# Dense peer experts: 48 first products ahead of the loop instead of 20, a third of all results kept in DRAM, and a gate stage without data work on GpSimd

## The chip, the cores and the metric

One core of a Trainium2 chip runs the whole program. The metric is the device time of one execution in microseconds (us). Five engines work side by side, each in its own order: TensorE (PE, with its weight loads as PEld), VectorE (DVE), ScalarE (ACT), GpSimd (POOL), and SyncE (SP), which here only starts transfers. Sixteen DMA engines move data between DRAM and the on-chip memory.

## The reference, cut to what matters

The program is two transformer blocks, one after the other, over 512 tokens of width 1024. The change lies in one part of the first block, the product-key layer `peer`:

```python
q = (nf @ w_q).reshape(t, PEER_HEADS, D_KEY)
...
v1, i1 = lax.top_k(s1, TOPK)
v2, i2 = lax.top_k(s2, TOPK)
...
idx = (e1 * N_KEYS + e2).reshape(t, PEER_HEADS * TOPK)
gates = jax.nn.softmax(vals.astype(jnp.float32), axis=-1).astype(n.dtype)
...
    ug = expert_u[ib]
    act = jax.nn.gelu(jnp.einsum("td,tkd->tk", xb, ug)) * gb
    vg = expert_v[ib]
    return jnp.einsum("tk,tkd->td", act, vg)
```

Each token picks 128 of 16384 small experts (8 heads, 16 each). An expert is a row of `expert_u` and a row of `expert_v`. The token's output is the sum over its experts of gelu(token . u) times the gate times v.

## The kernel before, in words

The kernel treats 384 of the 512 tokens (TD = 384, three tiles of 128) densely: it computes the product with all 16384 experts and multiplies by a gate matrix that is zero for the experts that a token did not choose. The experts are taken in 128 groups of 128. The last 128 tokens are treated sparsely: for each of the 128 chosen experts of every token, a gather fetches the rows (one indirect DMA of 128 rows of 4 KB, started by POOL; 128 gathers of u and then 128 of v), and DVE works on each.

All float32 products are split in a high and a low part: ACT writes the high part, the low part is the difference (`split`, L162), and three matmuls are summed (`mm3`, L175). The 16 top-k selections come first. Then these stages follow:

- **First products, S(e)** (`dense_s`, L693): load u of group e (tile ur), split it to uh and ul, 24 matmuls into a bank s, and gelu on ACT into a tile gl of [128 experts, 384 tokens]. Twenty of them (LAG) are made ahead of the loop: S(0) to S(7) as soon as the top-k is over, with the low part on POOL, six more between the gate calls, and six behind them.
- **Gate stage** (`decode`, `keys`, `gates`, L635 to L729): for each block of 4 tokens, DVE builds a one-hot tile gb (L717), and the weighted one-hot tile ga comes from a comparison on DVE for 8 tokens (eq, L710), times the gate, which is done by ACT (L722, four instructions) for three blocks in eight and by POOL (L724) for the other five. Four float32 matmuls (two PE instructions each) give the gate values of 4 tokens for all experts; ACT copies them into stg (L728). After eight blocks stg is stored to DRAM as gd (L729). There are 12 such calls, 96 blocks, 768 PE instructions.
- **Dense loop** (L565) over e = 0 to 127: **second product V(e)** (`dense_v`, L731) loads v of group e, splits it, multiplies gl[e] by the gates (gt, loaded from gd for four e at a time, L568), splits the result and adds 18 matmuls to six accumulators; then S(e + 20), while there is one; then gathers, so many that all 256 are through after 108 iterations (GSPAN). In this loop the order of the DVE instructions is the written one (`manual_schedule`). Elsewhere a scheduler, in the compiler, fixes each engine's order from the order of the program and its own estimate of times.

The first V needs the gates of all 12 calls. On SP all loads and the stores of gd stand in one queue. Buffers that matter: ur 3, uh 2, ul 2, ga 4, gb 2, bank s 2, bank b 4, vr 3, vh 2, vl 2, gr (gather) 4, gt 2.

Of the kernel before, what the change touches and what calls it, by code (L numbers as in the profile page):

```python
# [7 lines left out]
F32 = mybir.dt.float32  # L8
F32R = mybir.dt.float32r
BF = mybir.dt.bfloat16  # L10
I32 = mybir.dt.int32
U32 = mybir.dt.uint32
AF = mybir.ActivationFunctionType
# [5 lines left out]
T, D, NT, ND8 = 512, 1024, 4, 8  # L19
DT = 3  # L20
TD = DT * 128
LAG = 20
GSPAN = 108
GACT = (0, 3, 6)
NRAW, NRAW2 = 14, 3
CK, NSP, NDEP, POOLN = 2, 8, 5, 12
HEADS, TOPK, NK = 8, 16, 128
# [119 lines left out]
class Body:  # L147
# [331 lines left out]
    def peer(self, xst):  # L479
        tc, nc, A = self.tc, self.nc, self.A  # L480
        hT = self.hT
        gd = self.dram.tile([TD // 32, 128, 128, 32], F32, name="gd")
        with ExitStack() as st:
            pool = lambda **k: st.enter_context(tc.tile_pool(**k))
            np_ = pool(name="nhl", bufs=1)
# [20 lines left out]
                    nc.scalar.activation(n3[:, 512 * c:512 * c + 512], ps, AF.Copy)  # L506
            self.gl = {}
            S = lambda e, eng=None: self.dense_s(up, e, nh, nl, eng)
            ns = 0
            with tc.tile_pool(name="tk", bufs=1) as tk:  # L510
                v16 = tk.tile([128, 8, 4, 2, 16], F32, name="v16")
                i16 = tk.tile([128, 8, 4, 2, 16], U32, name="i16")
                w16 = tk.tile([128, 8, 4, 16], F32, name="w16")
                c16 = tk.tile([128, 8, 4, 16], U32, name="c16")
                with tc.tile_pool(name="p1", bufs=1) as p1, tc.tile_pool(name="p0", bufs=1) as p0:
                    for h in range(HEADS):
                        self.topk(p1, h, *self.xhl, v16, i16, w16, c16, (lambda: norm(p0)) if h == 0 else None)
                xst.close()
                ust = ExitStack()
                up = ust.enter_context(tc.tile_pool(name="up", bufs=1, side="right"))  # L520
                while ns < 8:
                    S(ns, nc.gpsimd)
                    ns += 1
                with tc.tile_pool(name="pg", bufs=1) as pg:
                    self.iota8 = pg.tile([128, 128, 8], BF, name="iota8")
                    nc.vector.tensor_copy(self.iota8, self.iota.rearrange("p (k o) -> p k o", o=1).to_broadcast([128, 128, 8]))
                    dec = self.decode(pg, i16, w16, c16, g3)
                    for t in range(NT):
                        tr = self.keys(pg, t, *dec, ix3)
                        if t < DT:  # L530
                            for q in range(4):
                                self.gates(pg, gd, 4 * t + q, tr, q)
                                if ns < LAG and q % 2:
                                    S(ns, nc.gpsimd if ns % 2 else None)
                                    ns += 1
            mst.close()
            while ns < LAG:
                S(ns)
                ns += 1
            with tc.tile_pool(name="pv", bufs=1) as pv:  # L540
                ast = ExitStack()
                ast.enter_context(self.banks(a=2 * DT))
                acc = [[self.bank("a") for c in range(2)] for t in range(DT)]
                dots = pv.tile([128, 128], F32, name="dots")
                o3 = pv.tile([128, 1024], F32, name="o3")
                scr = pv.tile([128, 1024], F32, name="scr")
                nc.vector.memset(o3, 0.0)

                def gather(j):
                    r = pv.tile([128, 1024], F32, name="gr", bufs=4)  # L550
                    if j == 128:
                        nc.scalar.activation(dots, dots, AF.Gelu_apprx_tanh)
                        nc.vector.tensor_mul(dots, dots, g3)
                    src, i = (A["u_r"], j) if j < 128 else (A["v_r"], j - 128)
                    nc.gpsimd.indirect_dma_start(out=r, out_offset=None, in_=src,  # L555
                                                 in_offset=bass.IndirectOffsetOnAxis(ap=ix3[:, i:i + 1], axis=0))
                    if j < 128:
                        nc.vector.tensor_tensor_reduce(scr, r, n3, op0=ALU.mult, op1=ALU.add, scale=1.0,  # L558
                                                       scalar=0.0, accum_out=dots[:, i:i + 1])
                    else:  # L560
                        nc.vector.scalar_tensor_tensor(o3, r, dots[:, i:i + 1], o3, op0=ALU.mult, op1=ALU.add)  # L561

                ng = 0
                with tc.manual_schedule(engines={mybir.EngineType.DVE}):
                    for e in range(128):  # L565
                        if e % 4 == 0:
                            gt = pv.tile([128, TD // 32, 4, 32], F32, name="gt", bufs=2)
                            nc.sync.dma_start(gt, gd[:, :, e:e + 4, :].rearrange("h p e t -> p h e t"))  # L568
                        self.dense_v(pv, e, gt, acc)
                        if e + LAG < 128:  # L570
                            S(e + LAG)
                        while ng < 256 and ng * GSPAN < 256 * (e + 1):
                            gather(ng)
                            ng += 1
                ust.close()
                self.early()

                for t in (3, 0, 1, 2):
                    if t < DT:
                        o = pv.tile([128, 1024], F32, name="gr", bufs=4)  # L580
                        for c in range(2):
                            nc.scalar.activation(o[:, 512 * c:512 * c + 512], acc[t][c], AF.Copy)
                    else:
                        o = o3
                    for c in range(2):
                        ps = self.bank("s")
                        for k in range(4):
                            i = 4 * c + k
                            nc.tensor.transpose(ps[:, 128 * k:128 * k + 128], o[:, 128 * i:128 * i + 128], self.ident)
                        h = hT[:, 4 * c:4 * c + 4, 128 * t:128 * t + 128]  # L590
                        nc.vector.tensor_add(h, h, ps.rearrange("p (k t) -> p k t", k=4))
                ast.close()
# [100 lines left out]
    def dense_s(self, up, e, nh, nl, eng=None):  # L693
        nc, A = self.nc, self.A
        uh, ul = self.load_split(up, [128, 8, 128], A["u_t"][e], "u", eng=eng)
        ps = self.bank("s")
        self.mm3(ps[:, :TD], lambda k: (uh[:, k], ul[:, k], nh[:, k, :TD], nl[:, k, :TD]), 8)
        g = up.tile([128, TD], F32, name="gl", bufs=LAG + 2)
        nc.scalar.activation(g, ps[:, :TD], AF.Gelu_apprx_tanh)
        self.gl[e] = g  # L700

    def gates(self, p, gd, th, tr, q):
        nc = self.nc
        tr, trb = tr
        stg = p.tile([128, 128, 32], F32, name="stg", bufs=2)
        for b in range(8):
            if b % 2 == 0:
                t = 32 * q + 4 * b
                eq = p.tile([128, 128, 8], BF, name="eq", bufs=3)
                nc.vector.tensor_tensor(eq, self.iota8, trb[:, t:t + 8].rearrange("p (o t) -> p o t", o=1).to_broadcast([128, 128, 8]),  # L710
                                        op=ALU.is_equal)
            t = 32 * q + 4 * b
            e = eq[:, :, 4 * (b % 2):4 * (b % 2) + 4]
            a = p.tile([128, 4, 128], F32, name="ga", bufs=4)
            bb = p.tile([128, 4, 128], F32, name="gb", bufs=2)
            ps = self.bank()
            nc.vector.tensor_tensor(bb, self.iota.rearrange("p (o k) -> p o k", o=1).to_broadcast([128, 4, 128]),  # L717
                                    tr[:, 1, t:t + 4].rearrange("p (t o) -> p t o", o=1).to_broadcast([128, 4, 128]),
                                    op=ALU.is_equal)
            if b % 8 in GACT:  # L720
                for i in range(4):
                    nc.scalar.activation(a[:, i], e[:, :, i], AF.Copy, scale=tr[:, 2, t + i:t + i + 1])  # L722
            else:
                nc.gpsimd.tensor_mul(a, e.rearrange("p k t -> p t k"),  # L724
                                     tr[:, 2, t:t + 4].rearrange("p (t o) -> p t o", o=1).to_broadcast([128, 4, 128]))
            for i in range(4):
                nc.tensor.matmul(ps[:, 128 * i:128 * i + 128], bb[:, i], a[:, i], start=True, stop=True)  # L727
            nc.scalar.activation(stg[:, :, 4 * b:4 * b + 4], ps.rearrange("p (t e) -> p e t", t=4), AF.Copy)  # L728
        nc.sync.dma_start(gd[th], stg)  # L729

    def dense_v(self, p, e, gt, acc):  # L731
# [811 lines left out]
```

## Time and profile before

| what | value |
|---|---|
| median of 3 runs | 3362.38 us (3360.96 to 3362.39) |
| the profiled execution, its own time | 3356.17 us |
| its span, first to last instruction | 3354.4 us |
| PE busy, share of the span | 94% |
| DVE / ACT / POOL busy | 80% / 52% / 30% |
| mean granted TensorE clock | 0.974 |
| gate stage with its first products, first S to first V | 365.0 to 635.6 us |
| dense loop | 635.6 to about 1607 us |

The stages are read by windows of the span, counted from its start; a busy share is that of one stretch, and the clock is the share of full speed that was granted in it. A busy PE is not always a PE at its peak, as the ends of matmuls are modelled; the spacing of the starts tells more than the length.

### The profile page before, as it was taken

What the parts mean: (1) busy time and instruction counts of PE and PEld (TensorE: products, weight loads), DVE (VectorE), ACT (ScalarE), POOL (GpSimd) and SP (SyncE); (2) the same over time, 40 slices, a digit from 0 to 9 for tenths busy, and PEclk for the clock granted to TensorE, in tenths of its full rate; (3) what the DMA queues carried; (4) which work ended last, traced back from release to release, by engine and by line L of the source; (5) the groups of instructions that cost most, each with busy time, mean ns of one, the idle gap of its engine ahead of it and who ended that gap; (6) DMA issues with size and microseconds to landing.
All of it is one profiled execution on the core that took longest, in us unless ns stands there. A gap on an engine that the chain in (4) does not pass through costs nothing. (4 is left out here: it accounts for less than half of the span.)

```text
span 3354.4 us, 44364 instructions
## 1 busy us (share of the span) xinstructions
PE 3139.9 (94%) x15489; PEld 2645.6 (79%) x15489; DVE 2679.3 (80%) x4138; ACT 1756.8 (52%) x2297; POOL 1014.4 (30%) x617
## 2 busy tenths in 40 slices
PE   8999877999999999999999898999999999999995
PEld 6777776899999999998777665777777777777774
DVE  8968889677777777775756745999998999999995
ACT  4232366433333333333545433677777777777774
POOL 0004355344444444440444213222222222222221
PEclk9999888999999999999999998999999999999998
DMA  4342223788888988984211335899999999999994
GB/s 139 98 132 78 85 120 161 293 305 304 301 304 299 309 305 299 306 283 150 101 61 41 104 105 200 321 341 334 337 340 348 339 343 336 334 339 344 339 343 152
DMA packets 280244, 819.30 MB, mean 244 GB/s; under 512 B 29648, under 2 KB 91984, under 8 KB 278224
## 3 DMA queue, kind: packets, MB, share of 16 engines
q1 hardware_dynamic: 223760, 659.09, 55.2%
q0 software_dynamic: 46080, 151.04, 13.8%
q10 hardware_dynamic: 10176, 6.29, 0.6%
q8 instruction: 123, 2.02, 0.2%
q14 instruction: 105, 0.86, 0.1%
HBM read 782.74 MB, written 50.33 MB: 248 GB/s over the span
## 5 line engine op out<-in xcount | busy, mean ns | idle before, releaser
L180 PE MATMUL s<-nh,uh 128*128 128x384 f32 x1024 | 350.4, 342 | 9.7 <-ACT uh L163 9.6
L182 PE MATMUL s<-nh,ul 128*128 128x384 f32 x1024 | 349.2, 341 | 3.4 <-POOL ul L164 2.7
L181 PE MATMUL s<-nl,uh 128*128 128x384 f32 x1024 | 348.0, 340 | 0.0
L163 ACT ACTIVATE vh<-vr 128x1024 fp32r<-128x1024 f32 x128 | 135.9, 1062 | 311.3 <-issue 291.3
L555 POOL DMA_INDIRECT gr<-in_u_r_dram,ix x128 | 192.4, 1503 | 260.6 <-DVE dots L558 222.9
L555 POOL DMA_INDIRECT gr<-in_v_r_dram,ix x128 | 195.4, 1527 | 250.0 <-DVE o L561 218.4
L745 PE MATMUL a<-vh,gh 128*128 128x512 f32 x768 | 236.6, 389 | 0.0
L745 PE MATMUL a<-vl,gh 128*128 128x512 f32 x768 | 236.4, 389 | 0.0
L745 PE MATMUL a<-vh,gll 128*128 128x512 f32 x768 | 236.3, 389 | 0.0
L164 DVE TENSOR_TENSOR ul<-ur,uh 128x1024 fp32r<-128x1024 f32 x117 | 144.4, 1234 | 100.3 <-ACT uh L163 100.3
L164 DVE TENSOR_TENSOR vl<-vr,vh 128x1024 fp32r<-128x1024 f32 x128 | 156.6, 1224 | 67.7 <-ACT vh L163 67.7
L180 PEld LDWEIGHTS s<-nh,uh 128*128 128x128 f32 x1024 | 195.7, 191 | 14.7 <-ACT uh L163 10.5
L163 ACT ACTIVATE gh<-gl 128x384 fp32r<-128x384 f32 x128 | 67.3, 526 | 262.6 <-DVE gl L736 262.6
L182 PEld LDWEIGHTS s<-nh,ul 128*128 128x128 f32 x1024 | 195.0, 190 | 4.7 <-POOL ul L164 3.7
L181 PEld LDWEIGHTS s<-nl,uh 128*128 128x128 f32 x1024 | 195.2, 191 | 4.0
L163 ACT ACTIVATE uh<-ur 128x1024 fp32r<-128x1024 f32 x128 | 135.2, 1056 | 75.6 <-PE s L181 62.6
L745 PEld LDWEIGHTS a<-vl,gh 128*128 128x128 f32 x768 | 144.2, 188 | 30.2
L745 PEld LDWEIGHTS a<-vh,gll 128*128 128x128 f32 x768 | 144.2, 188 | 29.9
L561 DVE SCALAR_TENSOR_TENSOR o<-gr,dots,o 128x1024 f32<-128x1024 f32 x128 | 164.1, 1282 | 3.8 <-DMA gr<-in_v_r_dram,ix 1.2
L558 DVE CUSTOM_DVE_ANT_0 scr<-gr,n 128x1024 f32<-128x1024 f32 x128 | 156.4, 1222 | 4.8 <-DMA gr<-in_u_r_dram,ix 2.3
L727 PE MATMUL b<-ga,gb 128*128 128x128 f32 x768 | 118.8, 315 | 44.2 <-DVE gb L717 34.8
L745 PEld LDWEIGHTS a<-vh,gh 128*128 128x128 f32 x768 | 142.6, 188 | 21.4
(6594 smaller groups left out, 9342.5 us busy)
## 6 DMA issues: line engine op xcount, KB each, us to landing
wr<-in_w_dram SPq DMA_DIRECT2D x768, 512.0 KB, 6.1
ur<-in_u_t_dram SPq DMA_DIRECT2D x128, 512.0 KB, 5.0
vr<-in_v_r_dram SPq DMA_DIRECT2D x128, 512.0 KB, 6.7
gd<-stg SPq DMA_DIRECT2D x12, 2048.0 KB, 6.9
gt<-gd SPq DMA_DIRECT2D x32, 768.0 KB, 9.4
wqr<-in_w_q_dram SPq DMA_DIRECT2D x16, 512.0 KB, 3.6
wir<-in_w_in_dram SPq DMA_DIRECT2D x15, 512.0 KB, 3.6
wlr<-in_w_in_dram SPq DMA_DIRECT2D x12, 512.0 KB, 3.7
```

Of the source, the lines that this page charges most:

```text
L163: self.nc.scalar.activation(hi, raw, AF.Copy)
L164: (eng or self.nc.vector).tensor_sub(lo, raw, hi.bitcast(F32))
L180: mm(ps, ah, bh, start=(k == 0 and start), stop=False)
L181: mm(ps, ah, bl, start=False, stop=False)
L182: mm(ps, al, bh, start=False, stop=(k == n - 1 and stop))
L555: nc.gpsimd.indirect_dma_start(out=r, out_offset=None, in_=src, in_offset=bass.IndirectOffsetOnAxis(ap=ix3[:, i:i + 1], axis=0))
L558: nc.vector.tensor_tensor_reduce(scr, r, n3, op0=ALU.mult, op1=ALU.add, scale=1.0, scalar=0.0, accum_out=dots[:, i:i + 1])
L561: nc.vector.scalar_tensor_tensor(o3, r, dots[:, i:i + 1], o3, op0=ALU.mult, op1=ALU.add)
L727: nc.tensor.matmul(ps[:, 128 * i:128 * i + 128], bb[:, i], a[:, i], start=True, stop=True)
L745: mm(acc[t][c], a[:, ts], v[:, 512 * c:512 * c + 512], start=(e == 0 and a is gh and v is vh), stop=(e == 127 and a is gl))
```

## The change

Forty-eight first products are made ahead of the loop. The groups 1, 4, 7, ... 118 (SPILL, 40 of 128) are all among them; the result of such a one is stored to a DRAM tensor gsd by a DMA that ACT starts, and loaded again by SP just ahead of its V, into one of three tiles gs. Of the other 88 (KEEP), the first 8 are made ahead and stay on chip as before. The first 8 of the 48 come right after the top-k, the other 40 are handed out one at a time behind single blocks of the gate stage (slots for 42, by `ahead`). No low part and no ga is made on POOL any more: the low part of u is always made on DVE; ga is made on ACT for four blocks in eight (from eq, 24 of which are left of 48) and on DVE for the other four (four `tensor_scalar` of [128, 128] each). In the loop only 80 S are left, none in the iterations of SPILL. Gathers are paced by the products done (128 V and 80 S, 208 in all) and are through after 88% of them.

```diff
-LAG = 20
-GSPAN = 108
-GACT = (0, 3, 6)
+LAG = 8
+SPILL = range(1, 120, 3)
+KEEP = [e for e in range(128) if e not in SPILL]
+GSPAN = 0.88
+GACT = (0, 1, 4, 5)
...
+        self.gsd = self.dram.tile([len(SPILL), 128, TD], F32, name="gsd")
...
+            it = iter([e for e in range(128) if e in SPILL or e in KEEP[:LAG]])
+            def ahead(b, q):
+                if b in ((0, 3, 6) if q % 2 else (0, 2, 4, 6)):
+                    e = next(it, None)
+                    if e is not None:
+                        S(e)
...
-                while ns < 8:
-                    S(ns, nc.gpsimd)
-                    ns += 1
+                for _ in range(8):
+                    S(next(it))
...
-                                self.gates(pg, gd, 4 * t + q, tr, q)
-                                if ns < LAG and q % 2:
-                                    S(ns, nc.gpsimd if ns % 2 else None)
-                                    ns += 1
+                                self.gates(pg, gd, 4 * t + q, tr, q, ahead)
...
-            while ns < LAG:
-                S(ns)
-                ns += 1
+            for e in it:
+                S(e)
...
+                ng, done, total = 0, 0, 128 + len(KEEP) - LAG
+                later = iter(KEEP[LAG:])
...
+                        if e in SPILL:
+                            self.gl[e] = up.tile([128, TD], F32, name="gs", bufs=3)
+                            nc.sync.dma_start(self.gl[e], self.gsd[SPILL.index(e)])
                         self.dense_v(pv, e, gt, acc)
-                        if e + LAG < 128:
-                            S(e + LAG)
-                        while ng < 256 and ng * GSPAN < 256 * (e + 1):
+                        done += 1
+                        s = next(later, None) if e in KEEP else None
+                        if s is not None:
+                            S(s)
+                            done += 1
+                        while ng < 256 and ng * GSPAN * total < 256 * done:
                             gather(ng)
...
+        if e in SPILL:
+            g = up.tile([128, TD], F32, name="gsp", bufs=3)
+            nc.scalar.activation(g, ps[:, :TD], AF.Gelu_apprx_tanh)
+            nc.scalar.dma_start(self.gsd[SPILL.index(e)], g)
+            return
...
-            if b % 2 == 0:
-                t = 32 * q + 4 * b
-                eq = p.tile([128, 128, 8], BF, name="eq", bufs=3)
+            if b in GACT and b % 2 == 0:
+                eq = p.tile([128, 128, 8], BF, name="eq", bufs=2)
...
-            if b % 8 in GACT:
-                for i in range(4):
-                    nc.scalar.activation(a[:, i], e[:, :, i], AF.Copy, scale=tr[:, 2, t + i:t + i + 1])
-            else:
-                nc.gpsimd.tensor_mul(a, e.rearrange("p k t -> p t k"),
-                                     tr[:, 2, t:t + 4].rearrange("p (t o) -> p t o", o=1).to_broadcast([128, 4, 128]))
+            for i in range(4):
+                if b in GACT:
+                    nc.scalar.activation(a[:, i], eq[:, :, 4 * (b % 2) + i], AF.Copy, scale=tr[:, 2, t + i:t + i + 1])
+                else:
+                    nc.vector.tensor_scalar(a[:, i], self.iota, tr[:, 0, t + i:t + i + 1], tr[:, 2, t + i:t + i + 1],
+                                            op0=ALU.is_equal, op1=ALU.mult)
...
+            ahead(b, q)
```

## Rows read from the trace of the kernel before

**Rows 1.** Tile vh: the matmuls of the loop; ns min/median/max, first and last start us.

```profile
L745 PE MATMUL a<-vh,gh x768: 389/389/391, 635.7 to 1606.8; 128*128 128x512 f32 x192
```

**Rows 2.** Windows: length; PE, PEld, DVE, ACT, POOL busy (instructions); clock; DMA share; GB/s.

```profile
400.00:600.00 200.00, 156.92 (x1029) 144.33 (x1028) 166.22 (x162) 126.56 (x253) 111.69 (x63) 0.88 0.34 136
650.00:1500.00 850.00, 850.00 (x4331) 777.74 (x4330) 656.79 (x784) 309.43 (x413) 374.62 (x246) 1.00 0.89 303
1550.00:1600.00 50.00, 50.00 (x222) 41.42 (x221) 27.59 (x37) 19.46 (x25) 0.00 (x0) 1.00 0.47 148
```

**Rows 3.** Groups of instructions, 360 to 640 us; busy us, mean ns, idle before.

```profile
L727 PE MATMUL b<-ga,gb 128*128 128x128 f32 x768 | 118.8, 315 | 44.2 <-DVE gb L717 34.8 <-ACT ga L722 8.4 <-POOL ga L724 0.7
...
L724 POOL TENSOR_TENSOR ga<-eq,tr 128x512 f32<-128x512 bf16 x60 | 100.6, 1688 | 69.8 <-PE b L727 57.0 <-DVE eq L710 12.5 <-POOL ga L724 0.3
L717 DVE TENSOR_TENSOR gb<-consts,tr 128x512 f32<-128x512 f32 x96 | 94.3, 1002 | 19.2 <-PE b L727 18.4
L722 ACT ACTIVATE ga<-eq,tr 128x128 f32<-128x128 bf16 x144 | 67.9, 520 | 14.5 <-DVE eq L710 14.5
...
L728 ACT ACTIVATE stg<-b 128x512 f32<-128x512 f32 x96 | 57.0, 595 | 54.3 <-PE b L727 54.0
L710 DVE TENSOR_TENSOR eq<-iota,trb 128x1024 bf16<-128x1024 bf16 x48 | 51.7, 1087 | 1.2 <-POOL ga L724 1.2
...
L163 ACT ACTIVATE uh<-ur 128x1024 fp32r<-128x1024 f32 x22 | 23.2, 1056 | 31.7 <-PE s L181 19.3 <-DMA ur<-in_u_t_dram 5.1 <-POOL ul L164 4.0
...
L699 ACT ACTIVATE gl<-s 128x384 f32<-128x384 f32 x20 | 9.6, 480 | 1.8 <-PE s L182 1.8
...
L665 DVE COPY g<-g 128x128 f32<-128x128 f32 x1 | 0.2, 227 | 0.0
```

**Rows 4.** Timeline, single lines of the gate stage: start us, length us, instruction.

```profile
417.67 0.68 DVE L717 TENSOR_TENSOR gb<-consts,tr 128x512 f32<-128x512 f32 x1
...
604.23 2.97 PEld L727 LDWEIGHTS b<-ga,gb 128*128 128x128 f32 x24 [0.72 <-POOL ga L724]
...
607.59 1.96 PE L681 MATMUL x<-oh,cb 128*128 128x128 bf16 x32
```

**Rows 5.** Timeline of PE and DVE where the first products begin; idle time in brackets.

```profile
365.04 0.69 PE L180 MATMUL s<-nh,uh 128*128 128x384 f32 x1 [5.04 <-ACT uh L163]
...
377.27 0.69 DVE L526 CAST iota<-consts 128x1024 bf16<-128x1024 f32 x1 [0.19 <-issue]
...
390.52 0.69 PE L180 MATMUL s<-nh,uh 128*128 128x384 f32 x1 [4.52 <-ACT uh L163]
...
398.69 0.37 PE L180 MATMUL s<-nh,uh 128*128 128x384 f32 x1
```

**Rows 6.** Timeline of SP and DVE from the last gate call to the first V.

```profile
608.05 0.32 SPq L729 DMA_DIRECT2D gd<-stg  x1
...
616.68 0.38 SPq L568 DMA_DIRECT2D gt<-gd  x1
...
629.20 0.56 DVE L164 TENSOR_TENSOR gll<-gl,gh 128x384 fp32r<-128x384 f32 x1 [0.59 <-ACT gh L163]
```

**Rows 7.** DMA queues, 650 to 1500 us: packets, MB, share of 16 engines.

```profile
q1 hardware_dynamic: 70040, 128.54, 44.6%
q0 software_dynamic: 35267, 128.41, 44.2%
```

**Rows 8.** One 4 us window of the loop; columns as in Rows 2.

```profile
728.00:732.00 4.00, 4.00 (x21) 3.54 (x20) 3.35 (x6) 1.06 (x1) 1.75 (x1) 1.00 1.02 398
```

**Rows 9.** DVE in the loop: two timeline lines, and one group of 650 to 1500 us.

```profile
701.79 0.56 DVE L164 TENSOR_TENSOR gll<-gl,gh 128x384 fp32r<-128x384 f32 x1 [0.65 <-ACT gh L163]
702.87 1.22 DVE L164 TENSOR_TENSOR ul<-ur,uh 128x1024 fp32r<-128x1024 f32 x1 [0.52 <-ACT uh L163]
...
L561 DVE SCALAR_TENSOR_TENSOR o<-gr,dots,o 128x1024 f32<-128x1024 f32 x124 | 159.0, 1282 | 3.7 <-DMA gr<-in_v_r_dram,ix 1.2
```

**Rows 10.** Source line L476: DMA starts on ACT's queue elsewhere in the kernel.

```profile
L476 ACTq DMA_DIRECT2D mvd<-mo x4: 326/326/327, 185.7 to 199.2; - x4
```

More of the change, by code (lines that the diff above doesn't have):

```diff
@@ L508, in peer @@
             S = lambda e, eng=None: self.dense_s(up, e, nh, nl, eng)
-            ns = 0
+            it = iter([e for e in range(128) if e in SPILL or e in KEEP[:LAG]])
[4 more added lines that the diff above has]
+                        S(e)
             with tc.tile_pool(name="tk", bufs=1) as tk:
@@ L561, in gather @@
                         nc.vector.scalar_tensor_tensor(o3, r, dots[:, i:i + 1], o3, op0=ALU.mult, op1=ALU.add)
-                ng = 0
+                ng, done, total = 0, 0, 128 + len(KEEP) - LAG
+                later = iter(KEEP[LAG:])
                 with tc.manual_schedule(engines={mybir.EngineType.DVE}):
@@ L700, in dense_s, with gates @@
         self.gl[e] = g
-    def gates(self, p, gd, th, tr, q):
+    def gates(self, p, gd, th, tr, q, ahead):
         nc = self.nc
@@ L706, in gates @@
         for b in range(8):
-            if b % 2 == 0:
-                t = 32 * q + 4 * b
-                eq = p.tile([128, 128, 8], BF, name="eq", bufs=3)
+            t = 32 * q + 4 * b
+            if b in GACT and b % 2 == 0:
+                eq = p.tile([128, 128, 8], BF, name="eq", bufs=2)
                 nc.vector.tensor_tensor(eq, self.iota8, trb[:, t:t + 8].rearrange("p (o t) -> p o t", o=1).to_broadcast([128, 128, 8]),
                                         op=ALU.is_equal)
-            t = 32 * q + 4 * b
-            e = eq[:, :, 4 * (b % 2):4 * (b % 2) + 4]
             a = p.tile([128, 4, 128], F32, name="ga", bufs=4)
```

## The prediction

> **What bounds the kernel now.** I first looked for the stage in which the change lies. The tile of v shows the dense loop: its first matmul starts at 635.7 us and its last at 1606.8 [rows 1], so the loop holds 971 of 3354 us. Then I took windows. In the loop with gathers PE is busy for all of 850 us at a granted clock of 1.00 (2.4 GHz) and DMA has a share of 0.89 [rows 2]: PE sets this stage's pace. In the gate stage PE is busy 157 of 200 us at a mean clock of 0.88, while DVE is busy 166 [rows 2]: here nobody is full, and PE waits. The groups of this stage say for whom: of 44.2 us idle ahead of gate matmuls, 34.8 ended with gb from DVE [rows 3], and DVE is slow because its gb takes 1.00 us in the mean [rows 3] against 0.68 where no POOL tensor work runs beside it [rows 4]. So work that moves from the loop to the gate stage leaves a full engine and meets a partly idle one, the same PE. The question is how much of its idle time can really be filled.
>
> **Unit prices.** At the end of the loop there are only second products: 222 matmuls in 50 us [rows 2], 18 for a V, so a V takes 4.05 us. The loop of 971.1 us has 128 V and 108 S; (971.1 - 128 x 4.05) / 108 gives 4.19 us for an S. Gate matmuls: 24 in 2.97 us [rows 4], so 768 take 95 us. The key matmuls: 32 in 1.96 us [rows 4], four times, 8 us.
>
> **The loop loses 28 S.** 108 become 80: 28 x 4.19 = -117.3 us, as long as PE stays the bound. What could take its place:
>
> DMA. The gathers now go into 88% of 208 steps (a step is a V or an S, 4.10 us in the mean), 183 steps or 751 us. The software queue was busy 44.2% of 850 us for 246 gathers [rows 7], 1.53 us each, so 256 need 391 us. The hardware queue moved 128.5 MB in 44.6% of 850 us [rows 7], 339 GB/s. In those steps it must move 0.88 x (208 x 0.524 + 32 x 0.786 + 40 x 0.197) = 125 MB, which is 369 us. Together 760 us of engine time in 751 us: full. On the other hand, in single windows of 4 us the queues move 398 GB/s at a share of 1.02 [rows 8], where the mean of the loop is 303 at 0.89 [rows 2]; so the price of a byte falls when the queues are full. 259 MB in 751 us are 345 GB/s, 87% of that window's rate.
>
> DVE. 656.8 us for 103 V and S and 246 gathers [rows 2]; a gather is one instruction of up to 1.28 us [rows 9]; what is left is 3.32 us for a V with its S, plus 0.65 us that DVE waits for ACT inside each V [rows 9]; the S in it is 1.22 us [rows 9]. In the 751 us stand 113 V, 70 S and 256 gathers: 113 x 2.75 + 70 x 1.22 + 256 x 1.28 = 724 us, 96%. In the 850 us of today it is (656.8 + 103 x 0.65) / 850 = 85%.
>
> Neither is above PE, both come close, and gathers have four buffers. Bounds: nothing, and 103 us (760 / 0.89 - 751, if the queues never get above today's share). I take 10, near nothing, because PE waited for no transfer at 0.89 and the 398 GB/s row shows room; DVE may run up to two V ahead of PE.
>
> The Trainium skill (HBM Reference, Specifications) gives a core about 358 GB/s as its share of the memory. By it the 345 GB/s of the gather steps would be 96% of what there is, and the second rival below, 3388, the likelier one. The 398 GB/s row speaks against it on a core that runs alone.
>
> **The stage ahead of the loop gains 28 S.** It lasts from the first S, 365.0 us [rows 5], to 635.7 [rows 1]: 270.7 us. PE's work in it at full speed was 20 x 4.19 + 95 + 8 = 187, so 84 us were lost. Afterwards the work is 48 x 4.19 + 95 + 8 = 304. To this I add three losses.
>
> Start. The low part of the first u moves from POOL to DVE, which is in the top-k until 377.3 us [rows 5]. PE's third matmul needs it (two can go ahead), so S begins in earnest at 378.5: 13 us.
>
> End. The first V needs gt, and gt needs the last stg: the store of gd is issued at 608.05, the load of gt at 616.68, and the last DVE step of V(0) starts at 629.20 [rows 6], 21 us after. Today six S cover this (6 x 4.19 = 25 us). Now the 42 slots take all 40 S, so none is left behind the gates, and an S of the loop can't step in: DVE's order in the loop is the written one, and its ul stands behind V(0). So 21 us of idle PE, and a slow start behind it: after an idle stretch of 4.5 us PE took from 390.5 to 398.7 us for S matmuls at half the clock (1.2 GHz) [rows 5], so about 4 us lost. Together 25.
>
> Between. PE waits for gb and ga. Below: nothing, as in the loop. Above: the busy share of today, 304 x (200 / 156.9 - 1) = 83 us. I take 22, half of the 44.2 us that gate matmuls wait now: two thirds of PE's work is now S, whose 24 matmuls run through, and while they run DVE and ACT get the next gb and ga ready, but gb has only two buffers.
>
> Are the others fast enough? DVE in the gate calls: 96 gb x 0.68 + 24 eq x 1.09 + 192 picks of [128, 128] at 0.23 (the copy of that size, [rows 3]) + 40 ul x 1.22 = 184 us. ACT: 192 x 0.52 + 57 (stg) + 40 x (1.06 + 0.48) [rows 3] + 40 DMA starts x 0.33 [rows 10] = 232 us. PE in the same calls: 95 + 40 x 4.19 = 263. So PE has the most. POOL's 60 products, 100.6 us [rows 3], are gone; that by itself gives nothing, as PE waited for POOL's ga in few cases, but gb gets its 0.68 us back. In ACT's queue a DMA start waits for the gelu of its own S, and the next stg or ga waits behind it for the 0.33 us; it is in the sum of ACT, which has 30 us to spare. On SP the 40 loads of gs stand ahead of loads of v, whose results are needed only an iteration later; their bytes are in the DMA sum. The stores to gsd, 8 MB, fall where DMA has a share of 0.34 [rows 2].
>
> The stage: 13 + 304 + 25 + 22 = 364 us, 93 more than 270.7.
>
> **Sum.** +93 - 117 + 10 = -14 us. The profiled execution took 3356.2 us, 6.2 less than the median shown. 3356.2 - 14 = 3342; on the scale of the median 3348.
>
> **Rivals.**
>
> *The gate stage leaks as it did* (slower). Same place, PE ahead of the gate matmuls, one cause: gb and ga come late because each engine's order is fixed beforehand and DVE has got 40 ul and 192 picks on top. For it: today PE idles a fifth of this stage even with fillers at hand. Against it: POOL no longer slows DVE, and S runs cover waits. It decides from a leak of 36 us on (22 + 14). At 70 us, nearer the 83 than the 22, the sum is +34: 3396.
>
> *DMA or DVE takes over the loop* (slower or no gain). For it: 760 us of engine time in 751 us, and a DVE at 96% which stops whenever a gather is late. Against it: the 398 GB/s row. It decides from 24 us of loss on; at 50 us, half of the upper bound, the sum is +26: 3388.
>
> *The losses cancel the gain*: leak and loop each some 7 us above my values, 3362, no change.
>
> *Nearly all holes are filled*: leak and loop loss at nothing, 13 + 304 + 25 = 342, +71 - 117 = -46: 3316.
>
> **How the numbers follow.** Within 0.2% is 6.7 us, about what a measurement can tell. Forecast and the fuller gain together 0.52 (all faster), cancelling 0.17, the leak 0.18, the loop 0.13 (both slower). So faster 0.52, same 0.17, slower 0.31. The time is that of the likeliest, 3348; its own range, for a leak of 5 to 30 and a loop loss of 0 to 20 us, is 3321 to 3366. The bounds of all unknowns together reach from 3316 to far above 3400; for 8 in 10 I leave out the worst of both slower cases: 3316 to 3396.
>
> **What the profile will show.** First V at about 729 us and last at about 1593. If the start loss is right, PE has a hole until some 378 us; if the end loss is, a hole of about 20 us stands before the first V, behind gt. gb should take 0.68 us all through the gate stage, and the clock there should be above 0.88. In the loop PE should be busy nearly all the time, with DMA above 0.95 during the gathers; waits of DVE for gr longer than some us in total would show the second rival. I would be wrong if S were still at work when the last gates are stored (the end loss gone), or if the first S waited longer than for the top-k.

## The result and the profile after

| what | before | after |
|---|---|---|
| median | 3362.39 us (4 runs, 3360.96 to 3363.05) | 3312.05 us (4 runs, 3308.80 to 3314.52) |
| the profiled execution | 3356.17 | 3314.52 |
| its span | 3354.4 | 3312.5 |

The ratio of after to before is 0.9851, 95% interval 0.9836 to 0.9865: the change makes the kernel 1.5% faster, 50 us by the medians, 42 us between the two profiled executions. 14 us were forecast. The direction was right; the time lies 4 us under the low end of the range.

Where the 42 us come from is read from the first and the last V, as in [rows 1]. Tile vh of the kernel after (ns min/median/max, first and last start us):

```profile
L761 PE MATMUL a<-vh,gh x768: 389/389/796, 700.5 to 1559.3; 128*128 128x512 f32 x192
```

From the first to the last V it is now 858.8 us, where [rows 1] had 971.1: 112.3 less (forecast: 107). The first V comes at 700.5, and the first S at 366.2 (below), so the stage ahead takes 334.3 us, where it took 270.6: 63.7 more (forecast: 93). The first S is 1.2 us later and the part behind the loop, whose code is the same, 5.6 us longer. 63.7 - 112.3 + 1.2 + 5.6 = -41.8. So the loop came out nearly as forecast and the stage ahead 30 us shorter.

Windows of the kernel after, columns as in [rows 2]: the stage, its middle without its two ends, and the loop with gathers.

```profile
366.20:700.50 334.30, 303.91 (x2055) 296.01 (x2055) 227.21 (x492) 213.44 (x400) 4.00 (x4) 0.96 0.53 188
400.00:680.00 280.00, 275.91 (x1901) 270.11 (x1900) 189.58 (x370) 194.49 (x377) 0.00 (x0) 1.00 0.55 193
720.00:1450.00 730.00, 728.40 (x3608) 652.54 (x3607) 612.04 (x758) 258.06 (x355) 367.97 (x246) 1.00 0.97 344
...
366.20:400.00 33.80, 24.49 (x120) 22.85 (x121) 33.51 (x115) 14.90 (x18) 0.00 (x0) 0.80 0.30 99
```

PE is busy for 303.9 us of the stage, and the work was put at 304. (The busy time contains a few matmuls at half the clock at the start, where the window reads 0.80.) PE idles for 30.4 us: 9.3 in the first 34 us, 4.1 in the 280 us of the middle, 17.0 at the end. In the middle the clock is 1.00 (2.4 GHz) throughout, where [rows 2] show 0.88 and 43 us idle in 200. In the loop PE loses 1.6 of 730 us, at a DMA share of 0.97 and 344 GB/s.

Groups of 360 to 702 us that answer to [rows 3] (busy us, mean ns, idle before):

```profile
L742 PE MATMUL b<-ga,gb 128*128 128x128 f32 x768 | 99.3, 278 | 2.5 <-ACT ga L737 2.0
...
L732 DVE TENSOR_TENSOR gb<-consts,tr 128x512 f32<-128x512 f32 x96 | 63.3, 687 | 11.0 <-PE b L742 10.7
...
L743 ACT ACTIVATE stg<-b 128x512 f32<-128x512 f32 x96 | 56.8, 595 | 6.9 <-PE b L742 5.6
L739 DVE TENSOR_SCALAR ga<-consts,tr 128x128 f32<-128x128 f32 x192 | 53.7, 343 | 0.0
...
L727 DVE TENSOR_TENSOR eq<-iota,trb 128x1024 bf16<-128x1024 bf16 x24 | 16.5, 687 | 2.3 <-ACT ga L737 2.3
```

The wait ahead of gate matmuls went from 44.2 to 2.5 us, gb from 1.00 to 0.69 us, and eq from 1.09 to 0.69. A pick of ga on DVE, one of the four `tensor_scalar`, takes 0.34 us where 0.23 was assumed; gb and the picks still come in time.

The two holes, in the timelines of PE, SP, ACT and DVE; they answer to [rows 5, 6]. (gh and gll are the high and the low part of gl times the gates, which V needs beside vh and vl.)

```profile
366.21 0.62 PE L182 MATMUL s<-nh,uh 128*128 128x384 f32 x1 [4.83 <-ACT uh L165]
...
375.89 0.69 PE L184 MATMUL s<-nh,ul 128*128 128x384 f32 x1 [7.47 <-DVE ul L166]
...
682.30 0.33 SPq L745 DMA_DIRECT2D gd<-stg  x1
689.63 0.38 SPq L574 DMA_DIRECT2D gt<-gd  x1
690.06 1.76 SPq L173 DMA_DIRECT2D vr<-in_v_r_dram  x3
...
696.62 1.06 ACT L165 ACTIVATE vh<-vr 128x1024 fp32r<-128x1024 f32 x1 [14.34 <-DMA vr<-in_v_r_dram]
699.01 1.06 ACT L165 ACTIVATE vh<-vr 128x1024 fp32r<-128x1024 f32 x1 [1.33 <-DMA vr<-in_v_r_dram]
699.97 0.51 ACT L165 ACTIVATE gh<-gl 128x384 fp32r<-128x384 f32 x1
...
700.51 0.56 DVE L166 TENSOR_TENSOR gll<-gl,gh 128x384 fp32r<-128x384 f32 x1 [1.11 <-ACT gh L165]
...
700.53 1.22 PE L761 MATMUL a<-vh,gh 128*128 128x512 f32 x2 [17.03 <-ACT gh L165]
```

Both stand where they were forecast. PE waits 7.5 us for the first ul, and 17.0 us from the last gates, whose store starts at 682.30, to the first V. The forecast had put this second wait on the store, the load of gt and the DVE steps behind it, but the rows show one more link. gt, issued at 689.63, landed after 5.5 us, at 695.1. The loads of v are issued only behind it, at 690.06, when SP has waited 7 us for the store. So the first v is there at 696.62, later than gt; the high part of the second v (699.01) stands ahead of gh in ACT's order, and gh is the step that ends PE's wait. What an earlier load of v would give was not run, and the memory of vr may itself be free only after that store: the clearing of o, a tile of the same pool, waited 6.5 us for it.

### The profile page after: what moved, and what is told of

Same layout as the page of the kernel before. It is cut to its first block, busy times and chain, and to the rows that moved or that the text cites. A ratio compares the mean times of both kernels' runs of the same rounds, so it can differ in the third digit from the quotient of the medians.

```text
span 3312.5 us, 44367 instructions
## 1 busy us (share of the span) xinstructions
PE 3122.0 (94%) x15489; PEld 2630.1 (79%) x15489; DVE 2650.0 (80%) x4317; ACT 1758.5 (53%) x2341; POOL 878.0 (27%) x546
## 5 line engine op out<-in xcount | busy, mean ns | idle before, releaser
L560 POOL DMA_INDIRECT gr<-in_u_r_dram,ix x128 | 185.2, 1447 | 529.2 <-issue 357.7
L166 DVE TENSOR_TENSOR ul<-ur,uh 128x1024 fp32r<-128x1024 f32 x128 | 156.2, 1221 | 77.1 <-ACT uh L165 77.1
L165 ACT ACTIVATE gh<-gl 128x384 fp32r<-128x384 f32 x88 | 46.2, 525 | 274.4 <-DVE gl L752 274.4
L761 PEld LDWEIGHTS a<-vl,gh 128*128 128x128 f32 x768 | 144.7, 188 | 30.4
L1418 ACT ACTIVATE ms<-mg 128x512 f32<-128x512 f32 x64 | 40.5, 633 | 200.2 <-DVE mg L1416 200.2
```

Source lines behind the costliest of these rows:

```text
L165: self.nc.scalar.activation(hi, raw, AF.Copy)
L166: (eng or self.nc.vector).tensor_sub(lo, raw, hi.bitcast(F32))
L761: mm(acc[t][c], a[:, ts], v[:, 512 * c:512 * c + 512], start=(e == 0 and a is gh and v is vh), stop=(e == 127 and a is gl))
L1418: nc.scalar.activation(s, g, AF.Sigmoid, scale=1.702)
```

## The experiments

There are two theories of why the leak is missing. A: POOL no longer works beside DVE, so gb comes in time. B: a first product now stands between most gate blocks and covers what is late. Two kernels make the missing corners of a square: POOL in the gate stage or not, 20 first products ahead or 48.

**POOL's ga put back, 48 first products kept.**

```diff
-GACT = (0, 1, 4, 5)
+GACT = (0, 3, 6)
...
-            if b in GACT and b % 2 == 0:
-                eq = p.tile([128, 128, 8], BF, name="eq", bufs=2)
+            if b % 2 == 0:
+                eq = p.tile([128, 128, 8], BF, name="eq", bufs=3)
...
+                nc.gpsimd.tensor_mul(a, e.rearrange("p k t -> p t k"),
+                                     tr[:, 2, t:t + 4].rearrange("p (t o) -> p t o", o=1).to_broadcast([128, 4, 128]))
```

> The changed kernel, but ga is made as in the kernel before (POOL for five blocks in eight, ACT for three, eq for every block); the 48 first products ahead, and their low parts on DVE, stay. Theory A: the leak vanished because POOL no longer works beside DVE, and gb is no longer slow. Then gb goes back to about 1.0 us, PE waits 20 to 44 us ahead of gate matmuls again, and the kernel takes 3332 to 3356 us. Theory B: the leak vanished because a first product stands between most of the gate blocks and covers the wait, whoever makes ga. Then gb may take 1.0 us all the same, PE waits less than 10 us ahead of gate matmuls, and the kernel takes 3310 to 3322 us.

Measured: 3328.1 us, ratio to before 0.9909 (0.9888 to 0.9930): between the two.

**The kernel before, with only the gate stage freed of POOL** (the edits of `gates` and of the low parts from the change; 20 first products, six of them behind the gates).

> The kernel before (20 first products ahead, nothing kept in DRAM), with its gate stage freed of POOL's data work as in the change: ga on ACT and DVE, low parts of u on DVE. Theory A (POOL's removal closed the leak): gb at about 0.69 us, the wait ahead of gate matmuls falls from 44 us to under 12, and the kernel takes 3325 to 3340 us. Theory B (the first products close it): with few of them between the gate blocks PE still waits 30 us or more, now for whatever is last of DVE and ACT, and the kernel stays within 3350 to 3375 us, with some 9 us lost at the start, where the first low part waits for DVE.

Measured: 3335.6 us, ratio 0.9933 (0.9916 to 0.9950): 22 us gained without one more first product ahead. Theory B alone is out; A alone is out as well by the kernel above. What came with POOL's absence is more than a faster gb: eq is needed half as often, and the low parts of u moved to DVE. The run doesn't separate these. Groups of the stage, first that kernel with POOL, then this one without:

```profile
L732 DVE TENSOR_TENSOR gb<-consts,tr 128x512 f32<-128x512 f32 x96 | 104.9, 1124 | 10.1 <-PE b L743 9.8
L743 PE MATMUL b<-ga,gb 128*128 128x128 f32 x768 | 98.9, 278 | 18.0 <-DVE gb L732 16.1 <-ACT ga L738 1.6
```

```profile
L725 PE MATMUL b<-ga,gb 128*128 128x128 f32 x768 | 125.4, 297 | 12.7 <-ACT ga L720 8.8 <-DVE gb L715 2.0 <-DVE ga L722 0.5
L715 DVE TENSOR_TENSOR gb<-consts,tr 128x512 f32<-128x512 f32 x96 | 65.5, 689 | 20.2 <-PE b L725 19.6
```

With windows of both stages (first S to first V; and the middle), again first the one with POOL:

```profile
366.50:718.90 352.40, 308.15 (x2055) 299.23 (x2055) 248.37 (x324) 194.67 (x352) 115.68 (x64) 0.96 0.51 179
...
400.00:700.00 300.00, 280.48 (x1898) 273.54 (x1897) 211.96 (x205) 176.05 (x329) 111.69 (x60) 0.99 0.52 180
```

```profile
365.70:610.60 244.90, 216.26 (x1380) 191.41 (x1381) 199.09 (x471) 166.98 (x340) 5.97 (x5) 0.96 0.45 170
...
400.00:580.00 180.00, 164.33 (x1109) 141.94 (x1107) 150.29 (x337) 145.40 (x311) 0.00 (x0) 0.99 0.39 156
```

The square, each cell with the stage's length, that length less the work (187 or 304 us), and the wait ahead of gate matmuls:

| | POOL in the gate stage | none |
|---|---|---|
| 20 ahead | 270.6; 84; 44.2 (before) | 244.9; 58; 12.7 |
| 48 ahead | 352.4; 48; 18.0 | 334.3; 30; 2.5 (after) |

POOL's absence is worth 26 us with 20 ahead and 18 with 48; the 28 first products take up 28 to 36 us of loss, by the column. The wait falls to 0.29 by the one, to 0.41 by the other, and to 0.06 by both, which is less still than the product (0.12). My half of 44 us was more than what either alone leaves. The square isn't quite clean: with 20 ahead six first products stand behind the gates and cover the end of the stage, with 48 none does, and in the kernel before some low parts are made on POOL too, which no other cell has. So the waits ahead of gate matmuls are the safer measure; the lengths contain these differences.

**How many first products are needed?** The changed kernel with 34 ahead, measured with the changed kernel itself on one chip.

```diff
-SPILL = range(1, 120, 3)
+SPILL = range(1, 128, 5)
...
-                if b in ((0, 3, 6) if q % 2 else (0, 2, 4, 6)):
+                if b in ((0, 4) if q else (0, 3, 6)):
```

> The changed kernel with 34 first products ahead of the loop instead of 48 (26 results kept in DRAM instead of 40), evenly handed out between the gate blocks, 14 more in the loop. Theory of filling: a first product costs the gate stage nothing as long as it goes into idle time of PE, and its full 4.19 us once PE is full; at 20 without POOL work the stage lost 58 us against its work, at 48 it loses 30, nearly all of it in the two holes at its ends. Then the first 14 fill nearly everything, and this kernel is within 6 us of the changed kernel. Rival, a cost that is even: each first product saves about 1.0 us (28 of them: 117 us less in the loop, 89 us more ahead of it), so that this kernel is 12 to 16 us slower than the changed one.

> The changed kernel itself, once more, as the common base for the three runs beside it, because four microseconds matter there. 3305 to 3314 us.

Measured: 3301.9 us (ratio to before 0.9837, 0.9816 to 0.9858) beside 3309.5 (0.9847, 0.9834 to 0.9861). No slower; by the intervals not faster either. The windows of 34 ahead, stage and middle:

```profile
367.30:643.60 276.30, 247.74 (x1719) 237.81 (x1719) 210.74 (x476) 194.78 (x372) 3.99 (x4) 0.96 0.53 190
...
400.00:620.00 220.00, 216.04 (x1529) 208.45 (x1528) 169.96 (x348) 171.71 (x341) 0.00 (x0) 1.00 0.55 199
```

Loss 276.3 - (34 x 4.19 + 95 + 8) = 31 us, as with 48, and 4.0 us of idle PE in the middle, as with 48. The theory of filling holds, and the even cost, which wanted this kernel 12 to 16 us slower, is out: the last 14 first products moved ahead gave nothing that these runs can show, they went from one full PE to another.

**The start.** `S(next(it), nc.gpsimd if i < 2 else None)` for the first eight: two low parts on POOL.

> The changed kernel, with the low parts of the first two u on POOL (2.34 us each there, while DVE is still in the top-k). If the start loss is the wait of the first low part for DVE, the 7.5 us hole in which PE waits for ul goes, and the kernel takes 3303 to 3308 us. Rival: the first products then run into the next wait, a load of u or the high part on ACT, and the time moves by less than 3 us.

Measured: 3303.5 us, ratio 0.9832 (0.9812 to 0.9853). The wait of 7.5 us became one of 1.4 for POOL, and a new one of 2.8 for DVE at the third u; the stage is 330.2 us, 4 shorter. About half of the hole was to be had. (The interval overlaps with that of the change, as does the next one; here the stage tells, which took 333.5 us when the changed kernel was measured again.)

**The end.** Four first products held back behind the last gates:

```diff
-                if b in ((0, 3, 6) if q % 2 else (0, 2, 4, 6)):
+                if b in (0, 3, 6):
```

> The changed kernel, with only 36 of the 40 first products handed out between gate blocks and four held back behind the last gates. If the hole of 17 us ahead of the first V is the end loss that the prediction named (store of gd, load of gt, first DVE steps), four first products, 16.8 us, cover it: PE works through, and the kernel takes 3293 to 3300 us. Rival: with four fewer fillers among the gates, PE waits there instead for gb and ga, since DVE and ACT need their time for the 96 blocks anyway; then the last gates come hardly earlier, and the time stays at 3308 to 3316 us.

Measured: 3300.6 us, ratio 0.9825 (0.9804 to 0.9845); its stage is 330.2 us (368.3 to 698.5), 4 us shorter where 17 were expected. The rival was wrong as well: PE waits only 3.0 us ahead of gate matmuls. Timelines of PE, SP and ACT:

```profile
672.72 0.33 SPq L745 DMA_DIRECT2D gd<-stg  x1
...
680.44 0.39 SPq L574 DMA_DIRECT2D gt<-gd  x1
680.87 2.63 SPq L173 DMA_DIRECT2D vr<-in_v_r_dram  x3
...
692.42 1.06 ACT L165 ACTIVATE vh<-vr 128x1024 fp32r<-128x1024 f32 x1 [5.00 <-DMA vr<-in_v_r_dram]
...
697.73 0.69 PE L182 MATMUL s<-nh,uh 128*128 128x384 f32 x1 [7.10 <-ACT gsp L712]
```

The gates were stored 10 us earlier, but the first V followed 26 us behind that store, not 18. DMA now carries u, the first gathers and v at once; v, issued at about 681, is ready only at 692.4; and on ACT the gelu of the last held product stands behind the high parts of two v, and gh of the first V behind that gelu, so PE has a hole of 7.1 us, ended by the gelu.

**Both holes at once**, with seven held back and the two low parts on POOL:

```diff
-                if b in ((0, 3, 6) if q % 2 else (0, 2, 4, 6)):
+                if b in ((0, 3, 6) if q < 3 else (0, 4)):
...
-                    S(next(it))
+                    S(next(it), nc.gpsimd if i < 2 else None)
```

> The changed kernel with both holes treated: the low parts of the first two u on POOL, and seven first products held back behind the last gates (33 between the blocks). With four held back the hole of 17 us shrank only to 7 us, because the path from the last gates to the first V itself grew from 18 to 26 us: transfers of u, of gathers and of v shared the queues (share 1.00 to 1.04), and on ACT the last held product stood behind the high part of the first v. Theory: seven (29 us) cover 26 us, no hole over 2 us is left, and the kernel is 16 to 22 us faster than the changed one. Rival: each further held product makes the path longer by its own transfers and its place on ACT; then a hole of 6 us or more stays, and the gain is 6 to 12 us.

Measured: 3285.1 us, ratio to before 0.9774 (0.9757 to 0.9792); the changed kernel on the same chip 3309.5. That is 24 us faster than the change, and faster than both kernels. The profiled spans are 22.9 us apart: 19.7 of them lie in this stage (333.5 us in the changed kernel measured again) and 3.8 behind the loop, in code that is the same. The stage:

```profile
367.30:681.10 313.80, 305.22 (x2051) 295.10 (x2052) 228.01 (x494) 209.62 (x396) 9.04 (x7) 0.99 0.57 204
```

313.8 us for 304 of work, clock 0.99. The hole of 17 us is gone (no wait of PE over 0.7 us is left between 655 us and the first V). So the loss at the ends was real, and most of it could be filled.

**How near is the loop to its edge?** All gathers are put into 70% of the products instead of 88 (`GSPAN = 0.70`).

> The changed kernel with all gathers in the first 70 per cent of the products instead of 88. Same bytes, in 598 us instead of 751: 259 MB would need 433 GB/s, above the 398 to 408 of the best 4 us windows, so the gathers must end the loop late at any theory of the queues. If the queues reach about 398 GB/s over the whole stretch, it takes 650 us and costs PE some 50 us there, of which DVE (724 us of work for what stands in 751 before, so also too much for 598) takes its own part: DVE needs 256 x 1.28 + 100 x 2.75 + 56 x 1.22 = 671 us for these steps, so the loss is 70 to 90 us: 3375 to 3405 us, set by DVE. If the memory gives no more than the 344 GB/s that the changed kernel showed, it takes 753 us: a loss of 150 us, 3455 to 3475 us. If PE loses under 20 us, both sums are wrong.

Measured: 3419.4 us, ratio 1.0179 (1.0163 to 1.0194): 110 us lost, between my two prices, so neither was the mechanism as priced. Two more kernels say more: one sends every third gather to one of two further buffers, the other lets DVE work on a quarter of each row.

```diff
-                    r = pv.tile([128, 1024], F32, name="gr", bufs=4)
+                    r = (up if j % 3 == 2 else pv).tile([128, 1024], F32, name="gr", bufs=2 if j % 3 == 2 else 4)
```

> The changed kernel with the gathers in 70 per cent of the products, and six gather buffers instead of four (every third gather goes to one of two further buffers). With four buffers the kernel took 3419 us, neither of the two prices given; DMA moved 325 GB/s at a share of 0.93, DVE was busy 78 per cent, POOL waited 237 of 560 us for DVE to free a buffer, and DVE 46 us for gathers. Theory of the round trip: four buffers, each 11 us under way (issue 1.4, landing 7.5, its turn and its 1.3 us on DVE), give a gather every 2.8 us, whatever the memory can do. Then six buffers bring the loop near what DVE's work allows, 671 us for this stretch: 3370 to 3390 us. Rival, the queues: they give no more, landing grows from 7.5 to 10 us or more as two more are under way, and the time stays at 3405 to 3425 us.

```diff
-                        nc.vector.tensor_tensor_reduce(scr, r, n3, op0=ALU.mult, op1=ALU.add, scale=1.0,
+                        nc.vector.tensor_tensor_reduce(scr[:, :256], r[:, :256], n3[:, :256], op0=ALU.mult, op1=ALU.add, scale=1.0,
...
-                        nc.vector.scalar_tensor_tensor(o3, r, dots[:, i:i + 1], o3, op0=ALU.mult, op1=ALU.add)
+                        nc.vector.scalar_tensor_tensor(o3[:, :256], r[:, :256], dots[:, i:i + 1], o3[:, :256], op0=ALU.mult, op1=ALU.add)
```

> The same 70 per cent, four buffers, but DVE works on 256 of the 1024 columns of each gathered row; three quarters of the sparse tokens' products are left out, the transfers are whole. DVE's part of a gather falls from 1.28 to some 0.35 us. If the transfers limit this stretch (259 MB), the time stays above 3390 us at the 325 GB/s seen, or, at the 398 of the best 4 us windows, is near 3360 us. If DVE's work and its order do (each late gather holds back the V behind it), the loop goes back to what PE needs, and the time is 3305 to 3325 us.

Measured: 3378.6 us with six buffers (ratio 1.0065, 1.0046 to 1.0084), 3338.4 with the light DVE (0.9944, 0.9928 to 0.9961). The same stretch of the loop, columns as in [rows 2], in four kernels: the changed one (measured again), 70%, 70% with six buffers, 70% with the light DVE:

```profile
720.00:1280.00 560.00, 558.17 (x2767) 500.37 (x2766) 469.09 (x611) 198.51 (x273) 283.42 (x190) 1.00 0.96 343
```

```profile
720.00:1280.00 560.00, 496.00 (x2322) 426.93 (x2321) 442.78 (x573) 169.16 (x228) 285.04 (x200) 0.97 0.93 325
```

```profile
720.00:1280.00 560.00, 520.14 (x2512) 451.72 (x2511) 479.98 (x609) 182.77 (x246) 294.67 (x215) 1.00 0.97 351
```

```profile
720.00:1280.00 560.00, 543.64 (x2653) 480.06 (x2652) 326.59 (x634) 186.43 (x261) 270.29 (x228) 1.00 1.00 371
```

DMA's rate was not what held the 70% kernel at 325 GB/s, as the light one moves 371 over all of 560 us. The theory of the round trip came true: with six buffers the median landing of a gather was 7.6 to 8.1 us, after 7.0 to 7.5 with four, and not the 10 of the rival, and the time lies in the range given. Six buffers take DVE's waits for gr from 46.7 us (32.2 + 14.5) to nothing, and DVE is still full: 480.0 busy plus 74.5 in which its gll waits for ACT's gh, inside a written order that lets nothing step in, is 554.5 of 560 us. (With four buffers it was 442.8 + 66.8 + 46.7 = 556.3.) The waits of DVE in that stretch, first with six buffers, then in the light kernel (scr and o are DVE's steps on a gathered row of u and of v; us in total, times, longest):

```profile
DVE gll L166 <- ACT gh L165: 74.5, 73, 1.8
```

```profile
DVE scr L563 <- DMA gr<-in_u_r_dram,ix: 92.0, 58, 4.0
DVE o L566 <- DMA gr<-in_v_r_dram,ix: 84.6, 51, 4.8
```

The light kernel's loop still takes 886 us (699.7 to 1586.0) where the changed one's takes 860. Its DVE waits 177 us for gr, so what is left there lies in the fetching of rows. Whether that is the rate, 371 GB/s at a share of 1.00, or once more the round trip of four buffers is not shown: a landing of 7.8, an issue of 1.2 and 0.5 us on DVE are 9.5 us, a quarter of which is 2.4, and a gather came every 2.5 us. A light kernel with six buffers was not run.

The changed kernel stands at the edge already. Its waits in the same stretch:

```profile
DVE gll L166 <- ACT gh L165: 53.7, 82, 0.9
...
DVE scr L563 <- DMA gr<-in_u_r_dram,ix: 22.4, 16, 2.8
DVE o L566 <- DMA gr<-in_v_r_dram,ix: 11.8, 10, 2.5
```

So 469.1 + 53.7 + 22.4 + 11.8 = 557 of 560 us of DVE are taken. PE still loses only 1.8 of these 560: as I read it, waits for gathers fill the time by which DVE is ahead of PE, and only what goes beyond it costs.

## Why the prediction was wrong, point by point

| term | forecast | measured |
|---|---|---|
| work of PE ahead of the loop (measured: busy) | 304 | 303.9 |
| start (measured: idle) | 13 | 9.3 |
| between (idle) | 22 | 4.1 |
| end (idle; the 25 hold 4 of slow start) | 25 | 17.0 |
| the stage | 364 | 334.3 |
| the loop, first to last V | -107 | -112.3 |

**The step that failed is "Between".** Its mechanism was right: PE waits for gb and ga, gb alone gets its 0.68 us back, and runs of S cover waits. Its size was not: 22 us were put down, and PE idled 4.1. That is 18 of the 30 us by which the stage was too long. I took half of the 44.2 us that today's gate matmuls wait, as if one remedy were applied. The change applies two, and the square shows that each alone cuts the wait to 12.7 or 18.0 us, both together to 2.5. I wrote that POOL's absence "by itself gives nothing" but gb's 0.68 us; the kernel before without POOL gained 22 us by that and what came with it. I also had the hint at hand: a DVE with 184 us and an ACT with 232 us of work beside a PE with 263 can run ahead, if nothing stalls them.

How POOL slowed DVE can be read from single instructions. One gb in the kernel with POOL's ga put back, and the product that POOL was making when it began:

```profile
519.97 1.72 POOL L740 TENSOR_TENSOR ga<-eq,tr 128x512 f32<-128x512 bf16 x1
520.50 1.74 DVE L732 TENSOR_TENSOR gb<-consts,tr 128x512 f32<-128x512 f32 x1
```

The product ends at 521.69, the gb 0.55 us later. In that kernel 57 of the 96 gb took 0.68 to 0.70 us; the other 39 took 1.49 to 1.80, each of them began while a product of POOL was under way, and each ended 0.55 to 0.56 us behind its end. Without POOL all 96 took 0.682 to 0.696. So a gb is either untouched or held until POOL is done. The Trainium skill (SBUF — State Buffer, Who interferes with whom) says that a VectorE instruction with two inputs in SBUF contends with a GpSimd instruction that reads SBUF, that the shared port is an exclusive lock, and that the order of issue decides who is blocked. The trace agrees: gb and ga have two inputs each, and POOL's products are held in the same way (last section).

**Start and end** were the right holes at the right places, 4 and 8 us too dear. The first ul was slotted in at 374.6 us ahead of the last of the top-k, where I had put it behind. At the end the path from the store of gd to the first gll took 18.2 us, where I had used the 21 of the kernel before, and the load that came last was v, not gt. The slow start behind it came as forecast, but falls into the loop: the first V took 5.9 us (700.5 to 706.4) instead of 4.05, so it cost 1.9 and not 4. The price of the gate matmuls was read from the row of their weight loads in [rows 4]; the matmuls were busy 99.3 us where 95 were put, which changes little.

**The loop.** PE set the pace, and the 10 us for DMA and DVE were too many: 112.3 us are gained where 117.3 were possible. The second rival was nearer than this looks: the sign that I named for it, waits of DVE for gr, did appear (44 us from 720 to 1450 us, where the kernel before had 1.2), but cost PE almost nothing. The sign was wrongly chosen. PE's own waits for gh are the better one: 1.4 us in that stretch, but 43.3, 17.9 and 16.1 us of the 560 in the three kernels at 70%.

My price of 50 us for that rival was put on DMA's rate. The kernels at 70% put its edge elsewhere first: on the round trip of four buffers and on DVE's written order with its waits, as six buffers gave back some 40 of the 110 us and the light DVE some 80. The Trainium skill (HBM Reference, Specifications) gives a core 358 GB/s as its share and says in the same section that a core alone gets well above it, about 425. I weighed the share only. The 371 GB/s over 560 us on a core that runs alone are above the share, as the second sentence has it; a rate near 425 no run here shows.

**The sum.** The stage was 29.7 us shorter than forecast and the loop gained 5.3 more; the shift of the first S and the part behind the loop take 6.8 back. That leaves 28.2, the distance from the forecast of about -14 to the -41.9 of the profiled spans. The part behind the loop isn't touched by the change; among kernels with the same code there it varied by 11 us (3313.5 - 1560.1 and 3300.0 - 1557.5). On the medians the gain is 50, because the profiled execution of before lay 6.2 under its median and that of after 2.5 above.

Of the rivals, "nearly all holes are filled" (3316) is the one that came nearest: the leak was 4.1 us and the loop's loss 5. The range ended at it, since I had kept start and end fixed at 13 and 25 us and varied only the leak and the loop.

Left open: in the two stages with 20 first products PE is also busy for some 30 us longer than its work at full speed (218 and 216 for 187 us), in those with 48 for 0 to 4. In the middle of the former the clocks are 0.88 and 0.99, so the clock is not all of it. Most of it stands in the gate matmuls, which are busy 118.8 [rows 3] and 125.4 us there and 98.9 and 99.3 with 48 ahead; in the kernel with 20 and no POOL the trace shows first products and gate matmuls in turn, a few at a time. Which of this costs how much wasn't separated.

## What to carry to other kernels

Work moved from a full engine into an engine's idle time is free until that idle time is used up, and then worth nothing: here 34 first products gave as much as 48, and the two holes at the ends, which the filler between the blocks can't reach, were worth some 20 us. When two remedies meet one wait, price each by itself and then both: here 0.29 and 0.41 of the wait were left by each and 0.06 by both, so half of it was far too much. Ahead of a stage that begins with a store, a load and a chain of small steps, keep more filler back than that path took before: here the filler's own transfers and its place on ACT lengthened it from 18 to 26 us. And look for what else is issued only behind that wait, as the loads of v were here.

## What the hardware showed that was not expected

- Between a gb and a POOL product the second to begin is held until the first is done: 39 of 39 gb ended 0.55 to 0.56 us behind the product that held them, where a gb takes 0.68 us alone. POOL's products are held as well. With 48 first products ahead, two that began beside no instruction of DVE took 1.30 us, those that began just behind the start of a ul 2.27 to 2.36. The mean there is 1.87, where half of them began beside a ul, and 1.69 with 20 [rows 3].
- DMA moved 371 GB/s at a share of 1.00 over 560 us; the share reads 0.93 at 325 and 0.96 to 0.97 at 343 to 351, so a share near 1 in the slower cases was not yet the limit.
- DVE at 84% busy (469 of 560 us) was in fact full: in a written order its waits for ACT and for gathers left 3 us.
